# First attention head prepared inside the query projection, later heads fetched two ahead: a diffusion trunk on one core

## The chip, the cores and the metric

The kernel runs on one core of one Trainium2 chip. The metric is the device time of one execution, in microseconds (us). All times below are in us from the start of the profiled span unless another unit stands there.

## What is computed

A trunk of two layers over 512 latent and 256 context tokens (together T = 768) of width 1024. Each layer projects its modulated input once; the columns feed three groups of heads (RWKV time mixing, attention, mLSTM), whose outputs are projected back together, and a SwiGLU feed-forward follows. The change touches the attention group and its neighbour, the mLSTM. Attention has 8 heads with keys of 96 channels; a query is projected from a normalized latent `cq`, normalized per head, rotated, and goes against all keys:

```
ql, kl, vl = project(zl, True)     # latent tokens, rotated
qc, kc, vc = project(zc, False)    # context tokens
keys = concat([kl, kc]); vals = concat([vl, vc])
s = einsum(q, keys) * (MLA_QK ** -0.5); p = softmax(s); out = einsum(p, vals)
out_c = attend(qc, kc, vc)         # only in the first layer
```

In the first layer queries are formed for all 768 tokens, in the last for the 512 latent ones.

## The kernel before

All matmul work that must be accurate is split in two parts, hi and lo, and takes three passes (L246 to L248, L1028 to L1030). The program is written with pools of tiles; a list scheduler decides the order on each engine from the program's dependences, and then every engine executes its list in order. DMAs go out from SP's list, also in order. A tile's memory or PSUM bank is handed to the next tile of the same name, in program order, when the last reader is done.

In each layer, after the RWKV scan, `mla_up` forms keys, queries and values while `mlstm` works on the side. `heads` projects pairs of token tiles (`up`, PSUM tile `up`, two of them), normalizes and rotates, and `by_channel` transposes four heads at a time into the PSUM tile `bc` (L904), ScalarE copies them to `stg` (L906, three buffers), and SP writes them to DRAM, to `ktd` or `qtd` (L907). First come the keys of all heads, then the queries of heads 0 to 3 (a = 0), then those of heads 4 to 7 (a = 1), then the values (`up` of 512 columns, stored in three pages, L969).

`mla_attend` then takes the heads one after the other. `load` reads a head's keys and queries from DRAM into a staging tile `kq` (two of them) and splits each: ScalarE rounds to hi (L993, L990), GpSimd (keys, L994) or VectorE (queries, L991, with the gain) forms lo. `maxima` finds the largest score of each query for the softmax: two matmuls into `mx` (L1008), a VectorE reduce (L1010), and after four query tiles a transposition into `pt` (L1014) and a copy to row 96 of the queries (L1015). `attend` forms the scores of 128 keys by 512 or 256 queries (`st`, L1028 to L1030), ScalarE takes the exponential (L1032), a matmul with the values adds to `po` (L1034). The first range of a head holds query tiles 0 to 3 against all keys, the second, only in the first layer, tiles 4 and 5 against the context's keys. At a range's end ScalarE copies the row of sums (L1039). The maxima of the next head are interleaved with the current one's keys, and its load is issued at the current one's start. After each of seven heads one piece of `rwkv_post` follows. The mLSTM's outputs lie in a page `hs` and its finish transposes them into `pss` (L1307).

Of the kernel before, what the change touches and what calls it, by code (L numbers as in the profile page):

```python
# [11 lines left out]
F32 = mybir.dt.float32  # L12
F32R = mybir.dt.float32r
# [13 lines left out]
POST = (0, 0, 0, 0, 0)  # L27
# [149 lines left out]
def trunk(ctx, tc, I, out, dbg=None):  # L177
# [662 lines left out]
    def mla_up(l, ctx_out, lat, wk, pm, krt, post, marks):  # L840

        steps = iter(POST)

        def fill():
            for _ in range(next(steps, 0)):
                next(post, None)
# [105 lines left out]
        fill()  # L952
        for n in range(0, NT, 2):
            heads(ckv, rkv, wt, n, n + 2, 8, 64, (kr2[:, :, 0], ks), ktd, 0)
            fill()
        for a in range(2):
            wt = up_weight("uq", 4, 384 * a, 384 * a + 384)
            for n in range(0, nq // P, QN):
                heads(cq, rq, wt, n, min(n + QN, nq // P), 4, 96, None, qtd, 4 * a)
            fill()  # L960
# [11 lines left out]
    def mla_attend(l, ctx_out, y, V, wk, wk2, pm, pv, post):  # L972
        nq = T if ctx_out else TL
        psum = lambda: pm.tile([P, 512], F32, name="mx")
# [5 lines left out]
        ac.activation(idr, ident, AF.Copy)  # L980

        def load(h):

            r = []
            for src, i, n in ((ktd, 1, T), (qtd, 0, nq)):
                t = wk.tile([96, T], F32, name="kq", bufs=2)[:, :n]
                dma = sp.dma_start(out=t, in_=src[h, :, :n])
                hi, lo = (w.tile([97, T], F32R, name=f"k{i}{j}", bufs=2)[:, :n] for j, w in enumerate((wk, wk2)))
                if i == 0:
                    ac.activation(hi[0:96], t, AF.Copy, scale=gain)  # L990
                    ve.scalar_tensor_tensor(lo[0:96], t, gain, hi[0:96].bitcast(F32), ALU.mult, ALU.subtract)  # L991
                else:
                    ac.activation(hi[0:96], t, AF.Copy)  # L993
                    gp.tensor_tensor(lo[0:96], t, hi[0:96].bitcast(F32), ALU.subtract)  # L994
                    gp.memset(hi[96:97].bitcast(F32), 1.0)
                r += [hi, lo]
            loads.append(dma)
            return r

        def maxima(kq, q0, q1, k0):  # L1000
            kh, kl, qh, ql = kq
            w = q1 - q0
            mr = wk.tile([P, 4], F32R, name="mr")
            for n in range(q0, q1):
                ps = pm.tile([P, 1024], F32, name="mx", bufs=1)
                for a, b in ((0, 512), (512, T)):
                    if a >= k0:
                        pe.matmul(ps[:, a - k0:b - k0], qh[0:96, n * P:(n + 1) * P], kh[0:96, a:b],  # L1008
                                  start=True, stop=True)
                ve.tensor_reduce(mr[:, n - q0:n - q0 + 1], ps[:, :T - k0], AX.X, ALU.max)  # L1010
                yield
            pt = pm.tile([P, 512], F32, name="pt")
# [3 lines left out]
            yield  # L1016

        def attend(h, kq, q0, q1, k0):
# [21 lines left out]
            pd = pm.tile([P, 512], F32, name="pt")  # L1040
# [4 lines left out]
            bc = pm.tile([P, 512], F32, name="pt")  # L1045
# [6 lines left out]
        ranges = ((0, 4, 0), (4, 6, 512))[:2 if ctx_out else 1]  # L1052
        loads, done = [], []
        kq = load(0)
        for _ in maxima(kq, *ranges[0]):
            pass
        for h in range(8):
            ahead = [maxima(kq, *g) for g in ranges[1:]]
            if h < 7:
                kq2 = load(h + 1)  # L1060
                ahead.append(maxima(kq2, *ranges[0]))
            ahead = chain(*ahead)
            for g in ranges:
                for _ in attend(h, kq, *g):
                    next(ahead, None)
# [6 lines left out]
            kq = kq2  # L1072
# [109 lines left out]
    def mlstm(l, ctx_out, y, qk, wk, pm, Q, rp):  # L1182
# [30 lines left out]
        hs = hp.tile([P, NT, 256], F32, name="hpage")  # L1213
# [9 lines left out]
        def chunk(d, i, n):  # L1223
# [12 lines left out]
            if has_y:  # L1236
# [34 lines left out]
                hv = hs[:, n].rearrange("p (h b) -> p h b", b=64)  # L1271
                rb = r.to_broadcast([P, 4, 64])
                if n in seen:
                    t = wk.tile([P, 4, 64], F32, name="m1")
                    ve.tensor_tensor(t, pn[:, :, 0:64], rb, ALU.mult)
                    gp.tensor_tensor(hv, hv, t, ALU.add)
                else:
                    seen.add(n)
                    ve.tensor_tensor(hv, pn[:, :, 0:64], rb, ALU.mult)
# [13 lines left out]
        def finish(ns):  # L1293

            st = wk.tile([P, 2, 8], F32, name="mst")
            for i, n in enumerate(ns):
                sq = wk.tile([P, 256], F32, name="m1")
                ac.activation(sq, hs[:, n], AF.Square)
                ve.tensor_reduce(st[:, 0, 4 * i:4 * i + 4], sq[:, :].rearrange("p (h b) -> p h b", b=64), AX.X, ALU.add)
            ve.tensor_scalar(st[:, 0], st[:, 0], 1.0 / 64, EPS, ALU.mult, ALU.add)  # L1300
            rsqrt(st[:, 1], st[:, 0], 8, "m")
            for i, n in enumerate(ns):
                hv = hs[:, n].rearrange("p (h b) -> p h b", b=64)
                ve.tensor_tensor(hv, hv, st[:, 1, 4 * i:4 * i + 4].unsqueeze(2).to_broadcast([P, 4, 64]), ALU.mult)
                ps = pm.tile([P, 512], F32, name="pss")
                for j in range(2):
                    pe.transpose(ps[:, j * P:(j + 1) * P], hs[:, n, j * P:(j + 1) * P], ident)  # L1307
# [79 lines left out]
    for l in range(DEPTH):  # L1387
# [24 lines left out]
        wp2 = rstack.enter_context(pool(f"po{l}", 2, "right"))  # L1412
        lstack = ExitStack()
        wm = lstack.enter_context(pool(f"ml{l}", 2, "right"))
        with pool(f"pb{l}", 1, space=PSUM) as psb, pool(f"pu{l}", 2, space=PSUM) as pm, \
                pool(f"mu{l}") as wk:
            marks = mlstm(l, ctx_out, y, qk, wm, psb, Q, rp)
            psum = [lambda: pm.tile([P, 512], F32, name="bc")]
            post = rwkv_post(l, ctx_out, data, y, wp2, psum)
            V = mla_up(l, ctx_out, lat, wk, pm, krt, post, marks)  # L1420
        lstack.close()
        with pool(f"ma{l}") as wk, pool(f"mb{l}") as wk2, pool(f"pv{l}", 2, space=PSUM) as pv, pool(f"pa{l}", 2, space=PSUM) as pm:
            psum[0] = lambda: pm.tile([P, 512], F32, name="pt")
            loads, marks = mla_attend(l, ctx_out, y, V, wk, wk2, pm, pv, post)
# [105 lines left out]
```

## Time and profile before

| | |
|---|---|
| runs shown | 2282.0 median of 3 (2281.18 to 2285.35) |
| profiled execution | 2283.55, span 2281.8 |
[...]
| busy: TensorE, VectorE, ScalarE, GpSimd | 2159.2, 1381.9, 844.7, 314.2 |
| TensorE waiting for the split of head 0 before its first maxima, layer 0 | 6.1 |

The page gives totals, costliest groups and the chain of work that ended last. The place of the change is short against the span, so it is read from views of a stretch: the chain of waits in it, a table by windows, and lists of single instructions. In a list, x2 behind a row means two instructions in a row, and brackets name what the engine had waited for. The engines are PE (TensorE), DVE (VectorE), ACT (ScalarE), POOL (GpSimd) and SP.

### The profile page before, as it was taken

To read this page: it belongs to the slowest core of one execution; us is meant where nothing else is said; L and a number is where in the kernel's file an instruction comes from. 1 tells how busy PE (TensorE), PEld (TensorE's weight loads), DVE (VectorE), ACT (ScalarE), POOL (GpSimd) and SP (SyncE) were. 2 spreads that over 40 slices of the span, in tenths; PEclk is the share of its full clock that TensorE was granted. 3 is DMA by queue.
4 is the path that set the end of the run, shared out by engine and by line. 5 is a ranking of instruction groups with operands and counts; after the bars stand their busy time and mean duration, and the time that the engine had idled before them with its cause. 6 is when DMAs were issued, how large, how long until landed. Compare 5 with 4: busy or idle time off the path is not lost.

```text
span 2281.8 us, 36365 instructions
## 1 busy us (share of the span) xinstructions
PE 2159.2 (95%) x14604; PEld 1780.9 (78%) x14604; DVE 1381.9 (61%) x2706; ACT 844.7 (37%) x1527; POOL 314.2 (14%) x482
## 2 busy tenths in 40 slices
PE   7999997997999999999999999999898998999999
PEld 4788886784668788888888878787685677888887
DVE  6687777895547766554444455788796545334343
ACT  4433333664552421122122354433473544222231
POOL 1022322332201100000000111113142211000000
PEclk9999997897999999999999989999697998999999
DMA  7241112232115334344432312211232122323323
GB/s 289 84 153 52 62 41 74 77 88 56 42 70 155 100 114 146 111 129 135 133 112 83 109 52 63 73 57 39 85 100 59 35 74 83 101 94 94 100 92 102
DMA packets 87352, 211.99 MB, mean 93 GB/s; under 512 B 10248, under 2 KB 33680, under 8 KB 86544
## 3 DMA queue, kind: packets, MB, share of 16 engines
q1 hardware_dynamic: 87184, 209.67, 29.2%
q8 instruction: 115, 1.88, 0.3%
q14 instruction: 53, 0.43, 0.1%
HBM read 187.62 MB, written 22.02 MB: 92 GB/s over the span
## 4 chain that ended last, share of the span: by engine, by line
PE 81%; DVE 10%; ACT 4%; DMA 2%; issue 2%; POOL 1%; SPq 0%; DVEq 0%; ACTq 0%; POOLq 0%
PE gm L262 57%; PE po L1034 4%; PE psm L585 2%; PE inv L660 2%; PE st L1028 1%; DVE cT L320 1%; PE st L1029 1%; PE st L1030 1%; PE mx L1008 1%; PE psm L514 1%; PE pB L700 1%; DVE wl L228 1%; PE psm L573 1%; ACT hu L365 1%; PE up L246 1%
## 5 line engine op out<-in xcount | busy, mean ns | idle before, releaser
L262 PE MATMUL gm<-hpage,wh 128*128 128x512 f32 (+1 forms) x3744 | 1001.7, 355 | 15.3 <-ACT hpage L227 8.9
L262 PEld LDWEIGHTS gm<-hpage,wh 128*128 128x128 f32 x3744 | 664.2, 191 | 119.8 <-ACT hpage L227 11.0
L262 PE MATMUL gm<-hpage,wl 128*128 128x512 f32 (+1 forms) x1872 | 657.4, 353 | 1.9 <-DVE wl L228 1.8
L227 ACT ACTIVATE wh<-wr 128x1024 fp32r<-128x1024 f32 (+2 forms) x214 | 221.6, 1036 | 560.7 <-PE gm L262 457.6
L262 PEld LDWEIGHTS gm<-hpage,wl 128*128 128x128 f32 x1872 | 358.1, 191 | 50.6 <-DVE wl L228 2.5
L228 DVE TENSOR_TENSOR wl<-wr,wh 128x1024 fp32r<-128x1024 f32 (+2 forms) x214 | 258.2, 1207 | 186.9 <-ACT wh L227 185.1
L262 PE MATMUL gm<-hid,wh 128*128 128x512 f32 (+1 forms) x1056 | 282.6, 356 | 0.0
L262 PEld LDWEIGHTS gm<-hid,wh 128*128 128x128 f32 x1056 | 185.6, 188 | 32.2
L262 PE MATMUL gm<-hid,wl 128*128 128x512 f32 (+1 forms) x528 | 187.4, 356 | 0.0
L1323 DVE SCALAR_TENSOR_TENSOR X<-gm,mod,X 128x512 f32<-128x512 f32 (+1 forms) x100 | 64.0, 643 | 191.0 <-PE gm L262 187.7
L320 DVE CUSTOM_DVE_ANT_0 cT<-wd,cB,mod_b 128x1024 f32<-128x1024 f32 x140 | 177.7, 1300 | 1.1 <-DMA wd<-in_mod_d 0.7
L1492 DVE SCALAR_TENSOR_TENSOR ft<-ft,gm 128x512 f32<-128x512 f32 x66 | 39.5, 598 | 153.0 <-PE gm L262 152.7
L1010 DVE TENSOR_REDUCE mr<-mx 128x1 fp32r<-128x768 f32 (+1 forms) x80 | 67.9, 848 | 83.8 <-PE mx L1008 83.6
L1034 PE MATMUL po<-pe,hpage 128*128 128x512 f32 (+1 forms) x224 | 112.2, 590 | 0.5 <-ACT pe L1032 0.4
L262 PEld LDWEIGHTS gm<-hid,wl 128*128 128x128 f32 x528 | 99.0, 188 | 16.1
L338 POOL TENSOR_TENSOR acc<-acc,sq 128x512 f32<-128x512 f32 (+1 forms) x15 | 23.9, 1601 | 604.0 <-ACT sq L337 604.0
L1032 ACT ACTIVATE pe<-st 128x512 f32<-128x512 f32 (+1 forms) x112 | 62.9, 563 | 89.8 <-PE st L1030 88.7
L227 ACT ACTIVATE hid<-ft 128x512 fp32r<-128x512 f32 x66 | 36.2, 549 | 128.4 <-DVE ft L1492 128.4
L1028 PE MATMUL st<-k,k 97*128 97x512 f32 (+1 forms) x112 | 78.0, 698 | 4.7 <-ACT k L1015 4.1
L1490 ACT ACTIVATE ft<-gm 128x512 f32<-128x512 f32 x66 | 33.9, 514 | 90.4 <-PE gm L262 90.3
L1008 PE MATMUL mx<-k,k 96*128 96x256 f32 (+1 forms) x144 | 46.3, 396 | 17.1 <-DVE mr L1010 9.9
L585 PE MATMUL psm<-pr,kb 64*128 64x128 f32 (+1 forms) x384 | 57.7, 308 | 1.4 <-POOL pr L555 1.4
(425 smaller groups left out, 3128.5 us busy)
## 6 DMA issues: line engine op xcount, KB each, us to landing
wr<-in_ffn_in SPq DMA_DIRECT2D x88, 512.0 KB, 3.5
wd<-in_mod_d SPq DMA_DIRECT2D x86, 512.0 KB, 3.8
wr<-in_w_in SPq DMA_DIRECT2D x44, 512.0 KB, 3.6
wr<-in_ffn_out SPq DMA_DIRECT2D x34, 448.0 KB, 3.4
wr<-in_w_out SPq DMA_DIRECT2D x20, 512.0 KB, 3.7
wr<-in_ffn_out SPq DMA_DIRECT2D x16, 512.0 KB, 3.6
zs<-ze SPq DMA_DIRECT2D x26, 256.0 KB, 2.0
X<-in_xT SPq DMA_DIRECT2D x16, 384.0 KB, 6.4
```

What stands on the lines that cost most here:

```text
L227: ac.activation(hi, src, AF.Copy)
L228: return en.tensor_tensor(lo, src, hi.bitcast(F32), ALU.subtract)
L262: pe.matmul(ps, x[:, j], act[k][y][:, a:b], start=(i == 0 and n == 0), stop=(i == len(kl) - 1 and n == 2))
L320: ve.tensor_tensor_reduce(out=t[:, s], in0=w, in1=cb[:, s], scale=1.0, scalar=modb[:, l, m:m + 1], op0=ALU.mult, op1=ALU.add, accum_out=mo ...
L585: pe.matmul(pa[j][:, p, c], flat(kb[hr, d, p, c]), flat(pr[hr, d, p, c, 0:nq]), start=True, stop=True)
L660: i = pe.matmul(v8(o)[hr, q], a[hr, d, p, c], b[hr, d, p, c], start=True, stop=True)
L1008: pe.matmul(ps[:, a - k0:b - k0], qh[0:96, n * P:(n + 1) * P], kh[0:96, a:b], start=True, stop=True)
L1010: ve.tensor_reduce(mr[:, n - q0:n - q0 + 1], ps[:, :T - k0], AX.X, ALU.max)
L1028: pe.matmul(ps, kh[0:97, ks], qh[0:97, qs], start=True, stop=False)
L1032: ac.activation(e, ps, AF.Exp, scale=QK_SCALE)
L1034: pe.matmul(po[:, :w], v, e, start=(kt == kts[0]), stop=(kt == kts[-1]))
L1323: return ve.scalar_tensor_tensor(X[:, m, a:b], ps, mods[l][:, 24 * which + 16 + m, s:s + 1], X[:, m, a:b], ALU.mult, ALU.add)
```

## The change

`mla_heads` now holds `load` and `maxima`, and a function `between` is called by `mla_up` after the queries of heads 0 to 3. It loads head 0's keys into a page (`hpage`) and its queries into a tile `qs` of a pool that is opened for it, splits them and takes the maxima of the first range, in the PSUM tiles `up` (512 and 256 columns apart, so eight reduces in place of four, and a maximum over the two) and `bc`. The load goes straight into the lo half of the tile, ScalarE forms hi from it, and lo is formed in place; the staging tile `kq` is gone. The keys and queries of later heads have three buffers, `ks` and `qs`, and are fetched two heads ahead. The mLSTM's outputs are stored in a part of `y`, which frees the page. The pool of `rwkv_post` (its loads of `g2` and `gz` among it) moves behind the mLSTM, and the pools of attention's PSUM tiles change places. Calls that were switched off (POST) are gone.

```diff
@@ mla_up
             for n in range(0, nq // P, QN):
                 heads(cq, rq, wt, n, min(n + QN, nq // P), 4, 96, None, qtd, 4 * a)
-            fill()
+            if a == 0:
+                between()
...
@@ mla_heads (new; load and maxima moved here)
+        def load(h, k, q):
+            kh, kl, qh, ql = k[0:97, 0], k[0:97, 1], q[0:97, 0, :nq], q[0:97, 1, :nq]
+            raw = lambda t: t[0:96].bitcast(F32)
+            sp.dma_start(out=raw(kl), in_=ktd[h])
+            ac.activation(kh[0:96], raw(kl), AF.Copy)
+            gp.tensor_tensor(kl[0:96], raw(kl), raw(kh), ALU.subtract)
+            gp.memset(kh[96:97].bitcast(F32), 1.0)
+            loads.append(sp.dma_start(out=raw(ql), in_=qtd[h, :, :nq]))
+            ac.activation(qh[0:96], raw(ql), AF.Copy, scale=gain)
+            ve.scalar_tensor_tensor(ql[0:96], raw(ql), gain, raw(qh), ALU.mult, ALU.subtract)
+            return kh, kl, qh, ql
...
             for n in range(q0, q1):
+                ps = None if mx is None else mx()
+                for i, (a, b) in enumerate(rng):
+                    p = psum("up")[:, :b - a] if mx is None else ps[:, a - k0:b - k0]
+                    pe.matmul(p, qh[0:96, n * P:(n + 1) * P], kh[0:96, a:b], start=True, stop=True)
+                    if mx is None:
+                        ve.tensor_reduce(m2[:, i, n - q0:n - q0 + 1], p, AX.X, ALU.max)
...
+            pt = psum("bc" if mx is None else "pt")
...
@@ mla_attend
-        kq = load(0)
-        for _ in maxima(kq, *ranges[0]):
-            pass
+        fetch = lambda h: load(h, wk.tile([P, 2, T], F32R, name="ks", bufs=3), wk2.tile([P, 2, T], F32R, name="qs", bufs=3))
+        kqs = {0: kq, 1: fetch(1)}
         for h in range(8):
-            ahead = [maxima(kq, *g) for g in ranges[1:]]
+            kq = kqs.pop(h)
+            ahead = [maxima(kq, *g, mx, psum) for g in ranges[1:]]
             if h < 7:
-                kq2 = load(h + 1)
-                ahead.append(maxima(kq2, *ranges[0]))
+                ahead.append(maxima(kqs[h + 1], *ranges[0], mx, psum))
+            if h < 6:
+                kqs[h + 2] = fetch(h + 2)
...
@@ mlstm
-        hs = hp.tile([P, NT, 256], F32, name="hpage")
+        hs = [y[:, 6:8, n * P:(n + 1) * P] for n in range(NT)]
...
@@ layer
-        wp2 = rstack.enter_context(pool(f"po{l}", 2, "right"))
+        qp = rstack.enter_context(pool(f"q{l}", 1, "right"))
+        heads, kq = mla_heads(l, ctx_out, qp), []
...
+            def between():
+                kq.append(heads[0](0, hp.tile([P, 2, T], F32R, name="hpage"), qp.tile([P, 2, T], F32R, name="qs")))
+                for _ in heads[1](kq[0], *RANGES[0], None, lambda name: pm.tile([P, 512], F32, name=name)):
+                    pass
+            V = mla_up(l, ctx_out, lat, wk, pm, krt, marks, between)
...
-        with pool(f"ma{l}") as wk, pool(f"mb{l}") as wk2, pool(f"pv{l}", 2, space=PSUM) as pv, pool(f"pa{l}", 2, space=PSUM) as pm:
+        with pool(f"po{l}") as wp2, pool(f"ma{l}") as wk, pool(f"mb{l}") as wk2, pool(f"pa{l}", 2, space=PSUM) as pm, pool(f"pv{l}", 2, space=PSUM) as pv:
```

The change moves instructions on every engine. TensorE's order in layer 0 of the kernel before, from the last values matmuls to the first scores (`bc` are transposed query pairs, `pss` the mLSTM's finish, `mx` the maxima):

```order
L248 MATMUL up<-wh,hpage 128x512
L904 MATMUL bc<-c_id,kn 96x128 x8
L1307 MATMUL pss<-c_id,hpage 128x128 x6
L1008 MATMUL mx<-k_5829,k_5836 128x512
L1008 MATMUL mx<-k_5829,k_5836 128x256
...
L1014 MATMUL pt<-idr,mr 128x128 x2
L1008 MATMUL mx<-k_5829,k_5836 128x256
L1028 MATMUL st<-k_5836,k_5829 128x512
```

And now, from the last query pair of heads 0 to 3 to the first matmuls of heads 4 to 7 (of 384 columns); `pn` and `pbc` are the mLSTM's chunks:

```order
L1236 MATMUL pbc<-c_id,sb 128x128
L898 MATMUL bc<-c_id,kn 96x128 x8
L1267 MATMUL pn<-C_4509,qd 128x260
L1270 MATMUL pn<-mva,m_4998 128x65 x4
...
L1270 MATMUL pn<-mva,m_5031 128x65 x4
L1313 MATMUL pss<-c_id,y 128x128 x2
L1002 MATMUL up<-hpage,qs 128x512
L1002 MATMUL up<-hpage,qs 128x256
L1313 MATMUL pss<-c_id,y 128x128 x2
...
L245 MATMUL up<-wh,hpage 128x384
L246 MATMUL up<-wl,hpage 128x384
```

Head 0's maxima stood between the values and the first scores, and stand now between the two halves of the query projection; all matmuls of heads 4 to 7 and of the values follow them, and the first scores follow the last `bc` directly.

ScalarE's order at the start of attention in layer 0, before (`kq` to `k` are the splits of heads 0 and 1, `pe` the exponentials):

```order
L906 ACTIVATE stg<-bc 96x512 x2
L980 ACTIVATE idr<-c_id 128x128
L993 ACTIVATE k_5829<-kq 96x768
L990 ACTIVATE k_5836<-kq,qkgain 96x768
L993 ACTIVATE k_5865<-kq 96x768
L990 ACTIVATE k_5872<-kq,qkgain 96x768
L1015 ACTIVATE k_5836<-pt 1x512
L1032 ACTIVATE pe<-st 128x512 x4
```

And now (`ks` are the keys of heads 1 and 2, then 3):

```order
L900 ACTIVATE stg<-bc 96x512 x2
L1036 ACTIVATE pe<-st 128x512 x2
L983 ACTIVATE ks<-ks 96x768 x2
L1036 ACTIVATE pe<-st 128x512 x2
L983 ACTIVATE ks<-ks 96x768
L1036 ACTIVATE pe<-st 128x512 x2
```

The splits of head 0 are gone from the start, and the copies of two later heads' keys stand between the second and the third exponential.

SP's order now, from the load of head 0's keys on (head 0's queries and those of heads 1 to 3 are the x4):

```order
L982 DMA hpage<-ktd 96x768
L901 DMA qtd<-stg 96x4x128 x2
L234 DMA wr<-in_ukv 128x2x512
L901 DMA qtd<-stg 96x4x128 x2
L234 DMA wr<-in_w_out 128x1024
L901 DMA qtd<-stg 96x4x128 x2
L986 DMA qs<-qtd 96x768 x4
L901 DMA qtd<-stg 96x4x128 x2
L234 DMA wr<-in_w_out 128x1024 x2
L901 DMA qtd<-stg 96x4x128 x4
L234 DMA wr<-in_w_out 128x1024
L982 DMA ks<-ktd 96x768 x2
```

All loads of a head stood behind the last query write; now the queries of four heads are read before the second half is written, while the keys of heads 1 and 2 still stand behind it.

## Rows read from the trace of the kernel before

**Rows 1.** The page: busy time of TensorE, share of the span, instructions; shares of the chain.

```profile
PE 2159.2 (95%) x14604; PEld 1780.9 (78%) x14604; DVE 1381.9 (61%) x2706; ACT 844.7 (37%) x1527; POOL 314.2 (14%) x482
...
PE 81%; DVE 10%; ACT 4%; DMA 2%; issue 2%; POOL 1%; SPq 0%; DVEq 0%; ACTq 0%; POOLq 0%
```

**Rows 2.** Chain of waits, layer 0, 509 to 535: start us, us, what.

```profile
509.43 0.23 PE up L247
...
509.90 0.87 PE bc L904 x8
...
514.04 6.21 DMA kq<-ktd
...
521.06 0.94 ACT k L990
...
523.85 3.23 DMA kq<-qtd
...
533.86 0.76 PE st L1028
```

**Rows 3.** Table by windows: stretch, length, busy us (and instructions) by engine, PEclk, DMA share, GB/s.

```profile
390.00:400.00 10.00, 4.95 (x68) 4.01 (x68) 7.02 (x15) 2.48 (x4) 1.27 (x5) 0.63 0.70 223
400.00:410.00 10.00, 9.42 (x85) 7.87 (x86) 6.74 (x13) 5.59 (x10) 1.33 (x1) 0.50 0.43 150
520.00:530.00 10.00, 3.24 (x8) 2.16 (x8) 6.02 (x8) 3.50 (x4) 3.62 (x2) 0.50 0.24 65
```

**Rows 4.** List of TensorE's instructions, layer 1, at 1738: start us, us, engine, line, operation.

```profile
1738.44 1.19 PE L1028 MATMUL st<-k,k 97*128 97x512 f32 x2 [0.16 <-ACT k L1015]
```

**Rows 5.** Lists of ScalarE's (row L1039) and TensorE's instructions, heads of both layers.

```profile
547.58 0.59 ACT L1039 ACTIVATE row<-po 1x512 f32<-1x512 f32 x1 [0.42 <-PE po L1034]
...
566.28 0.59 ACT L1039 ACTIVATE row<-po 1x512 f32<-1x512 f32 x1 [0.63 <-PE po L1034]
...
582.65 0.59 ACT L1039 ACTIVATE row<-po 1x512 f32<-1x512 f32 x1 [0.42 <-PE po L1034]
...
586.44 0.47 PE L1028 MATMUL st<-k,k 97*128 97x512 f32 x1 [0.58 <-ACT k L1015]
...
599.08 0.59 ACT L1039 ACTIVATE row<-po 1x512 f32<-1x512 f32 x1 [0.76 <-PE po L1034]
...
1753.87 0.59 ACT L1039 ACTIVATE row<-po 1x512 f32<-1x512 f32 x1 [0.60 <-PE po L1034]
...
1772.47 0.59 ACT L1039 ACTIVATE row<-po 1x512 f32<-1x512 f32 x1 [0.61 <-PE po L1034]
...
1786.12 0.59 ACT L1039 ACTIVATE row<-po 1x512 f32<-1x512 f32 x1 [0.60 <-PE po L1034]
```

**Rows 6.** List of SP's DMA issues: the query writes of both layers.

```profile
487.69 3.40 SPq L907 DMA_DIRECT2D qtd<-stg  x4
...
1706.05 1.35 SPq L907 DMA_DIRECT2D qtd<-stg  x2
```

**Rows 7.** DMA issues from 465 to 535: count, KB each, median us to landing.

```profile
qtd<-stg SPq DMA_DIRECT2D x12, 192.0 KB, 2.3
...
kq<-ktd SPq DMA_DIRECT2D x3, 288.0 KB, 4.6
kq<-qtd SPq DMA_DIRECT2D x3, 288.0 KB, 3.2
```

**Rows 8.** Groups of VectorE's instructions by shape, 425 to 560: busy us, mean ns.

```profile
L1010 DVE TENSOR_REDUCE mr<-mx 128x1 fp32r<-128x768 f32 x9 | 8.6, 953 | 11.8 <-PE mx L1008 11.8
...
L991 DVE SCALAR_TENSOR_TENSOR k<-kq,qkgain,k 96x768 fp32r<-96x768 f32 x3 | 4.3, 1449 | 2.9 <-ACT k L990 2.9
...
L1010 DVE TENSOR_REDUCE mr<-mx 128x1 fp32r<-128x256 f32 x4 | 1.7, 421 | 4.5 <-PE mx L1008 4.5
```

**Rows 9.** List of TensorE's instructions, second half of the query projection, layer 0.

```profile
485.40 0.33 PE L247 MATMUL up<-wl,hpage 128*128 128x384 f32 x1
...
485.75 0.33 PE L246 MATMUL up<-wh,hpage 128*128 128x384 f32 x1
```

More of the change, by code (lines that the diff above doesn't have):

```diff
@@ L26 @@
 EB = 6
-POST = (0, 0, 0, 0, 0)
 POSTA = (1, 1, 1, 1, 1, 1, 1, 0)
@@ L838, in latent, with mla_up @@
         return parts, rs
[L840 to L846, printed above, removed]
+    def mla_up(l, ctx_out, lat, wk, pm, krt, marks, between):
         nq = T if ctx_out else TL
@@ L970, in mla_up, with mla_heads @@
         return V
-    def mla_attend(l, ctx_out, y, V, wk, wk2, pm, pv, post):
+    RANGES = ((0, 4, 0), (4, 6, 512))
+    def mla_heads(l, ctx_out, wk):
         nq = T if ctx_out else TL
-        psum = lambda: pm.tile([P, 512], F32, name="mx")
         qkg = const("qkg", wk)
@@ L980, in mla_attend @@
         ac.activation(idr, ident, AF.Copy)
[L982 to L998, printed above, removed]
@@ L1000, in maxima @@
-        def maxima(kq, q0, q1, k0):
+        loads = []
+        def load(h, k, q):
[9 more added lines that the diff above has]
+            return kh, kl, qh, ql
@@ L1001, in maxima @@
+        def maxima(kq, q0, q1, k0, mx, psum):
             kh, kl, qh, ql = kq
             w = q1 - q0
-            mr = wk.tile([P, 4], F32R, name="mr")
+            mr = wk.tile([P, 4], F32R, name="mr", bufs=2)
+            rng = [(a, b) for a, b in ((0, 512), (512, T)) if a >= k0]
+            m2 = wk.tile([P, 2, 4], F32, name="m2", bufs=1) if mx is None else None
             for n in range(q0, q1):
[L1005 to L1010, printed above, removed]
+                ps = None if mx is None else mx()
[4 more added lines that the diff above has]
+                        ve.tensor_reduce(m2[:, i, n - q0:n - q0 + 1], p, AX.X, ALU.max)
+                if mx is not None:
+                    ve.tensor_reduce(mr[:, n - q0:n - q0 + 1], ps[:, :T - k0], AX.X, ALU.max)
@@ L1011, in maxima @@
                 yield
-            pt = pm.tile([P, 512], F32, name="pt")
+            if mx is None:
+                ve.tensor_tensor(mr[:, :w], m2[:, 0, :w], m2[:, 1, :w], ALU.max)
+            pt = psum("bc" if mx is None else "pt")
             for n in range(w):
@@ L1016, in maxima, with mla_attend @@
             yield
+        return load, maxima, loads
+    def mla_attend(l, ctx_out, y, V, heads, kq, wk, wk2, pm, pv, post):
+        load, maxima, loads = heads
+        psum = lambda name: pm.tile([P, 512], F32, name=name)
+        mx = lambda: pm.tile([P, 1024], F32, name="mx", bufs=1)
         def attend(h, kq, q0, q1, k0):
@@ L1039, in attend @@
             ac.activation(row, po[o:o + 1, :w], AF.Copy)
-            pd = pm.tile([P, 512], F32, name="pt")
+            pd = psum("pt")
             for n in range(q1 - q0):
@@ L1044, in attend @@
             ve.reciprocal(r[:, :q1 - q0], pd[:, :q1 - q0])
-            bc = pm.tile([P, 512], F32, name="pt")
+            bc = psum("pt")
             for n in range(q1 - q0):
@@ L1278, in chunk @@
                     seen.add(n)
-                    ve.tensor_tensor(hv, pn[:, :, 0:64], rb, ALU.mult)
+                    ve.tensor_tensor(hv, nv, rb, ALU.mult)
             if i == NT - 1:
@@ L1417, in trunk @@
             marks = mlstm(l, ctx_out, y, qk, wm, psb, Q, rp)
-            psum = [lambda: pm.tile([P, 512], F32, name="bc")]
-            post = rwkv_post(l, ctx_out, data, y, wp2, psum)
-            V = mla_up(l, ctx_out, lat, wk, pm, krt, post, marks)
+            def between():
[3 more added lines that the diff above has]
+            V = mla_up(l, ctx_out, lat, wk, pm, krt, marks, between)
         lstack.close()
-        with pool(f"ma{l}") as wk, pool(f"mb{l}") as wk2, pool(f"pv{l}", 2, space=PSUM) as pv, pool(f"pa{l}", 2, space=PSUM) as pm:
-            psum[0] = lambda: pm.tile([P, 512], F32, name="pt")
-            loads, marks = mla_attend(l, ctx_out, y, V, wk, wk2, pm, pv, post)
+        with pool(f"po{l}") as wp2, pool(f"ma{l}") as wk, pool(f"mb{l}") as wk2, pool(f"pa{l}", 2, space=PSUM) as pm, pool(f"pv{l}", 2, space=PSUM) as pv:
+            post = rwkv_post(l, ctx_out, data, y, wp2, [lambda: pm.tile([P, 512], F32, name="pt")])
+            loads, marks = mla_attend(l, ctx_out, y, V, heads, kq[0], wk, wk2, pm, pv, post)
         rstack.close()
```

25 lines of the change are left out of this document (12 added, 13 removed).

## The prediction

> **What bounds the kernel now.** I read the page first: TensorE is busy for 95% of the span and the chain that ends last runs over it for 81% [rows 1]. So a microsecond is won only where TensorE stands idle or runs slowly, and I looked for such places next to the code that changes. The chain of waits around the start of attention in layer 0 shows one: the transposes of the last query pair (bc) are issued at 509.90 and the first score matmul (st) at 533.86, and between them stand the DRAM round trip of head 0 (keys 6.21, queries of head 1 3.23), the splits and the maxima [rows 2]. In this stretch VectorE and ScalarE wait too; it is latency and not work. [...] In layer 1 the first st comes at 1738.44 [rows 4].
>
> The list of ScalarE's instructions gives the heads, by the copy of the sums' row that ends each head's first range. Layer 0: the first head takes 547.58 − 533.86 = 13.7, the second 18.7, the third 16.4. Layer 1: 15.4, 18.6, 13.65 [rows 4, 5]. An undisturbed head needs 599.08 − 586.44 = 12.6 from its first st to its row [rows 5]. [...]
>
> **The change, term by term.** All sums are in the profiled execution's own time, 2283.55; the median of the runs shown, 2282.0, is 1.55 lower. A measurement of this kernel tells 0.2%, 4.6 us, from no change.
>
> *1. First st of layer 0.* The round trip of head 0 isn't removed, it is moved between the two halves of the query projection. The maxima now write into the PSUM tiles named up and bc, and these are handed out in program order: the matmuls of the second half stand behind the maxima in TensorE's order and need the same two up tiles. So TensorE still waits for the trip, but with four chunks of the mLSTM to work on. When does the trip end? The queries of the last pair of the first half are written at 487.69 [rows 6]; the new order has that pair at about the same place, so I take 487.5. The write lands 2.3 later, the read of a head's queries 3.2 later [rows 7], ScalarE's half of the split takes 0.94 [rows 2], VectorE's 1.45, and then eight reduces in place of four: 0.95 for 768 columns and 0.42 for 256 [rows 8], so about 0.68 for 512 and 1.1 per tile, 4.4 in all. That is 499.9; VectorE has mLSTM work between, for which I add 1: 501. Behind it TensorE has 72 matmuls of the second half at 0.175 (two steps between starts in 0.35 [rows 9]), 36 for the values at 0.23 and 24 transposes at 0.11 (0.87 for eight) [rows 2], and 1.5 for the mLSTM's last transposes and the second range's maxima: 12.6 + 8.3 + 2.6 + 1.5 = 25. First st at 526 against 533.86. The bounds: a trip with the same contention as the chain shows (6.21 in place of 3.2) gives 529; a trip wholly inside the mLSTM's work, with the second half beginning at 495, gives 520.
>
> After the hold the clock has to be reckoned with. A stretch in which TensorE works little is followed by one at 0.50: at 390 to 400 it is busy for 4.95, and from 400 to 410 the clock is 0.50, though the engine is busy for 9.42 [rows 3]. Between nothing and 10 us at half rate, that is between 0 and 5 us lost, I take 2 a layer, nearer the low end, since the mLSTM's matmuls go on during the hold. [...] With 2: first st at 528.3, **−5.5**.
>
> *2. The first head of layer 0.* It now begins at full clock behind dense matmuls, 12.6. But it gets a new wait. The keys of head 2 are read behind the last query writes, because their new tile takes over memory of stg, and ScalarE has the copies of heads 1 and 2 ahead of its third exponential. From the last eviction, which also releases the first st: write 2.3, read 4.6 [rows 7], two copies 0.9 each: the third exponential at about 8 after the first st, where it would come at about 4.5. That holds ScalarE, then TensorE, for 3.3. What is queued behind it: the remaining exponentials, and with them every po matmul. With 0.3 for the clock, 16.2 against 13.7: **+2.5**. Bounds: 0 if the reads are as short as 3.2 and the copies overlap; +6 with a read of 6.21 and a restart at half rate.
>
> *3. The second head of layer 0.* Its loads come two heads ahead, so it costs a steady 16.4 and not 18.7: **−2.3**. A low clock behind the stall of term 2 could eat this, so 0 to −2.3.
>
> *4. Layer 1, first st.* The second pair of the first half is written at 1706.05 [rows 6]; without the second half's matmuls among it I take 1704. Then 2.3 for the write, 3.9 for the read (the middle of 3.2 and 4.6) [rows 7], 2 for the split, 4.4 for the reduces: 1716.6. Behind it 48 × 0.175 + 36 × 0.23 + 16 × 0.11 + 1.5 = 19.9, and 2 for the clock: 1738.5, and 1 more because the mLSTM ends late in this layer and VectorE was busy nearly to the first st. 1739.6 against 1738.44: **+1.2**, between −6 and +6.
>
> *5. Layer 1, first and second head.* 16.2 against 15.4 is **+0.8** (from −2.8 to +4.3, as term 2), and 13.7 against 18.6 is **−4.9** (0 to −4.9).
>
> *6. The small edits.* The gain and the maxima's bias are computed from the same number of columns; eight more reduces (2 x 4 x 0.15) lie in terms 1 and 4. The g2 and gz loads move behind the keys' loads and are used only in the second head; covered by term 2's wait, and without that cover one load of about 4. The mLSTM keeps its outputs in y and not in a page: same counts and same columns, so nothing. From the third head on the order of TensorE and ScalarE is nearly the old one, nothing. X is still loaded behind the fourth head's loads, and the weights of wd go ahead of it on SP's queue; the out-projection starts on y, so nothing, at worst one load of 4.
>
> Sum: −5.5 + 2.5 − 2.3 + 1.2 + 0.8 − 4.9 = **−8.2**. 2283.55 − 8.2 = 2275.35, on the median's footing 2273.8; I say **2274**.
>
> **The rivals.**
>
> *The hold vanishes.* If the mLSTM's chunks cover the trip wholly in both layers, the first st follows the last bc: about 512 in layer 0 (−22), and about 1732 in layer 1, where VectorE's remaining work sets it (−6). With terms 2, 3 and 5 as above: −22 + 0.2 − 6 − 4.1 = −32, so 2250. For it: the order puts mLSTM chunks into the gap. Against it: all of the second half's 72 matmuls stand behind the maxima, so 25 us of TensorE remain after the trip whatever covers it. Chance 0.07.
>
> *Moved, not won.* Terms 1, 2, 4 and 5 each lean to their dear ends by some 2: the read of head 0's queries shares the queues with 512 KB of w_out, as in the chain of before, and ScalarE waits for the third head's queries before the value weights are split. −8.2 + 4 × 2 = 0, so 2282. For it: the total wait per layer is the same DRAM trip twice, and term 2 adds a new one. Chance 0.23.
>
> *Slower by the clock.* [...] At 17 of the 25 us in each layer it is 8.5 and not 2, −8.2 + 13 = +4.8 in the profiled time: 2288, on the median's footing 2287; that is the point from which it is slower by more than 0.2%. [...] Chance 0.12.
>
> *The fetch two ahead does nothing,* if the copies' places in ScalarE's order hold it back: then terms 3 and 5 lose their 7.2 and the time is 2281. It counts with "moved, not won".
>
> **How the numbers follow.** The forecast, from 2262 to 2277.4, has 0.58, so faster by over 0.2% (under 2277.4) has 0.58 + 0.07 = 0.65. Within 0.2% has 0.23 and slower 0.12. The range reaches down to where about half of the first rival is out, 2259, and up to 2287, where the slower rival begins; some 0.15 is left out.
>
> **What would show it.** Right: the st that followed ACT k at 533.86 follows the last stg at 526 to 530; in 490 to 501 VectorE's reduces from up tiles, and the second half's first matmul waits for one; the third exponential of the first head waits for a copy of keys, which waits for a DMA from ktd; rows of head 2 − head 1 near 16.4 and 13.7. Wrong: second-half matmuls before 495; the first head at 12.6 without an idle ScalarE (better); a granted clock under 0.7 in 500 to 515 or 1716 to 1730 (worse); or heads from the third on that differ by over 0.3 each, which no term here explains.

## The result and the profile after

The changed kernel is slower: 2305.09 us (median of 4, 2298.69 to 2312.87) against 2283.68 (2281.18 to 2286.15), ratio 1.0097 with the interval 1.0076 to 1.0118. The forecast was 2274, with 2287 as the upper end of the range. The profiled execution is the slowest of the four, 2312.87, span 2310.9, 29.1 longer than the span of before.

The page of the changed kernel, busy time and shares of the chain, answers to [rows 1]:

```profile
PE 2179.3 (94%) x14604; PEld 1793.4 (78%) x14604; DVE 1381.1 (60%) x2716; ACT 846.9 (37%) x1527; POOL 311.1 (13%) x482
...
PE 80%; DVE 10%; DMA 4%; ACT 4%; issue 2%; SPq 0%; POOL 0%; ACTq 0%; DVEq 0%; POOLq 0%
```

The amount of work is the same, 14604 matmuls; TensorE's busy time grew by 20.1 and the span by 29.1. To see where, I take three marks in each layer from the lists of TensorE's instructions: the first matmul of the key projection (up), the first scores (st) and the first matmul of the output projection (gm). The kernel before, the marks not shown above:

```profile
422.08 0.48 PE L246 MATMUL up<-wh,hpage 128*128 128x512 f32 x1
...
673.20 0.96 PE L262 MATMUL gm<-hpage,wh 128*128 128x512 f32 x4 [0.29 <-ACT hpage L227]
...
1654.82 0.48 PE L246 MATMUL up<-wh,hpage 128*128 128x512 f32 x1
...
1854.35 0.70 PE L262 MATMUL gm<-hpage,wh 128*128 128x512 f32 x2
```

The changed kernel:

```profile
424.70 0.48 PE L245 MATMUL up<-wh,hpage 128*128 128x512 f32 x1
...
536.61 0.50 PE L1032 MATMUL st<-qs,hpage 97*128 97x512 f32 x1 [1.81 <-ACT stg L900]
...
681.26 0.96 PE L261 MATMUL gm<-hpage,wh 128*128 128x512 f32 x4 [1.13 <-ACT hpage L226]
...
1663.01 0.48 PE L245 MATMUL up<-wh,hpage 128*128 128x512 f32 x1
...
1756.24 0.50 PE L1032 MATMUL st<-qs,hpage 97*128 97x512 f32 x1 [1.29 <-ACT stg L900]
...
1882.70 0.50 PE L261 MATMUL gm<-hpage,wh 128*128 128x512 f32 x1 [0.85 <-DVE y L1054]
```

From the first up to the first st it is 111.8 before [rows 2] and 111.9 now in layer 0, 83.6 [rows 4] and 93.2 in layer 1. From there to gm it is 139.3 and 144.7 in layer 0, 115.9 and 126.5 in layer 1. The stretch from gm of layer 0 to up of layer 1 is 981.6 and 981.8. So layer 1 costs some 20 and layer 0 some 5.5; 2.6 lie ahead of the first up and 0.7 after the last gm. The medians differ by 21.4 and not by 29.1; in which stretch this execution is slower than the median one isn't known.

The copies of the sums' row that end the first heads, as in [rows 5]:

```profile
554.14 0.59 ACT L1043 ACTIVATE row<-po 1x512 f32<-1x512 f32 x1 [0.42 <-PE po L1038]
...
571.91 0.59 ACT L1043 ACTIVATE row<-po 1x512 f32<-1x512 f32 x1 [0.47 <-PE po L1038]
...
1769.86 0.59 ACT L1043 ACTIVATE row<-po 1x512 f32<-1x512 f32 x1 [1.59 <-PE po L1038]
```

The first head takes 17.5 in layer 0 and 13.6 in layer 1 (13.7 and 15.4 before), the second 17.8 and 18.8 (18.7 and 18.6).

**The hold in layer 1.** The chain of waits of the changed kernel, 1690 to 1800 (start, us, what):

```profile
1714.05 1.72 PE bc L898 x8
...
1716.41 2.18 DMA qtd<-stg
1718.73 2.38 DMA qs<-qtd
...
1726.94 1.03 PE pn L1267 x2
...
1730.88 0.69 PE up L245
...
1740.97 1.07 ACT wh L226
...
1743.32 0.35 SPq L234
1743.71 4.71 DMA qs<-qtd
...
1750.53 0.50 PE up L245
```

The last query pair of heads 0 to 3 is transposed at 1714.05, written and read again, and only at 1730.88 does the second half start: 16.8 us. Between the maxima (up L1002 in the chain) stands a chunk of the mLSTM (pn). After this comes a second hold that I hadn't priced: SP's queue waits at 1743.32 to issue a load of w_out into a buffer that VectorE must free first, the queries of heads 1 to 3 stand behind it (4.71), and ScalarE has their copies ahead of a values copy (hpage), so TensorE's next values matmul of the chain starts at 1750.53, after 0.98 of idle time.

The clock in the holds (table by windows, columns as in [rows 3]):

```profile
500.00:510.00 10.00, 7.81 (x24) 6.21 (x25) 7.55 (x27) 1.07 (x3) 0.72 (x1) 0.55 0.00 0
...
1720.00:1730.00 10.00, 8.48 (x29) 6.90 (x30) 7.69 (x32) 1.33 (x3) 2.16 (x4) 0.54 0.05 16
...
1740.00:1750.00 10.00, 9.29 (x46) 7.25 (x44) 8.53 (x27) 6.71 (x11) 2.01 (x3) 1.00 0.56 160
```

The granted clock was 0.55 in 500 to 510 and 0.54 in 1720 to 1730, though TensorE was busy for 7.81 and 8.48 of 10, and it was back at 1.00 by 1740. So TensorE had the low clock during the hold itself, while it worked on the mLSTM. The second half of layer 1 starts with it too: its first matmuls follow each other at 0.32, with a granted clock of 0.50 in 1730 to 1734, the later ones at 0.175, with 1.00 in 1735 to 1740.

**The second half in layer 0.** VectorE's list shows the splits of three later heads' queries inside the projection, among the second half's own work:

```profile
518.48 1.58 DVE L988 SCALAR_TENSOR_TENSOR qs<-qs,qkgain 96x768 fp32r<-96x768 f32 x1
...
521.12 1.00 DVE L988 SCALAR_TENSOR_TENSOR qs<-qs,qkgain 96x768 fp32r<-96x768 f32 x1
...
522.12 1.01 DVE L988 SCALAR_TENSOR_TENSOR qs<-qs,qkgain 96x768 fp32r<-96x768 f32 x1
```

**The first head of layer 0.** ScalarE's list:

```profile
537.60 1.29 ACT L1036 ACTIVATE pe<-st 128x512 f32<-128x512 f32 x2 [1.05 <-PE st L1034]
543.99 0.84 ACT L983 ACTIVATE ks<-ks 96x768 fp32r<-96x768 f32 x1 [5.10 <-DMA ks<-ktd]
545.23 0.84 ACT L983 ACTIVATE ks<-ks 96x768 fp32r<-96x768 f32 x1 [0.39 <-DMA gz<-zs]
545.98 1.06 ACT L1036 ACTIVATE pe<-st 128x512 f32<-128x512 f32 x2
```

The third exponential (the row of 545.98, two of them) waits for two key copies, and the first of these for a DMA, 5.10. This is the new wait of term 2.

**The later heads of layer 1.** ScalarE's list at the end of the second head:

```profile
1784.47 0.60 ACT L1036 ACTIVATE pe<-st 128x512 f32<-128x512 f32 x1 [1.42 <-PE st L1034]
1787.79 0.84 ACT L983 ACTIVATE ks<-ks 96x768 fp32r<-96x768 f32 x1 [2.73 <-DMA ks<-ktd]
1788.66 0.59 ACT L1043 ACTIVATE row<-po 1x512 f32<-1x512 f32 x1
```

The keys that are fetched two ahead are copied directly in front of the row copy, after a wait of 2.73 for their DMA. The row copy needs nothing from it and had no idle time of its own before it: it stood behind. The chain of waits shows what the DMA itself waited for, the last score matmul that reads the tile's old contents:

```profile
1784.20 0.24 PE st L1034
1784.51 3.20 DMA ks<-ktd
1787.79 0.84 ACT ks L983
1788.66 0.60 ACT row L1043
```

SP's queue says the same for the heads of layer 1 (its waits: us in total, times, longest):

```profile
SPq L982 <- PE st L1034: 67.6, 4, 22.0
```

The same pattern follows at later heads; summed over the heads of layer 1 (waits of ScalarE: us in total, times, longest):

```profile
ACT ks L983 <- DMA ks<-ktd: 11.2, 7, 2.7
```

The kernel before has no such wait behind the first head of layer 1: its DMA went to a staging tile.

### The profile page after: what moved, and what is told of

Read it like the earlier page. It is cut to its first block, busy times and chain, and to the rows that moved or that the text cites. A ratio compares the mean times of both kernels' runs of the same rounds, so it can differ in the third digit from the quotient of the medians.

```text
span 2310.9 us, 36349 instructions
## 1 busy us (share of the span) xinstructions
PE 2179.3 (94%) x14604; PEld 1793.4 (78%) x14604; DVE 1381.1 (60%) x2716; ACT 846.9 (37%) x1527; POOL 311.1 (13%) x482
## 4 chain that ended last, share of the span: by engine, by line
PE 80%; DVE 10%; DMA 4%; ACT 4%; issue 2%; SPq 0%; POOL 0%; ACTq 0%; DVEq 0%; POOLq 0%
PE gm L261 57%; PE po L1038 4%; PE psm L584 2%; PE inv L659 2%; DVE cT L319 1%; PE st L1032 1%; PE psm L513 1%; PE st L1033 1%; PE st L1034 1%; PE pB L699 1%; DMA wd<-in_mod_d 1%; PE mx L1002 1%; DVE wl L227 1%; PE psm L572 1%; PE up L245 1%
## 5 line engine op out<-in xcount | busy, mean ns | idle before, releaser
L261 PEld LDWEIGHTS gm<-hpage,wh 128*128 128x128 f32 x3744 | 663.8, 191 | 120.5 <-ACT hpage L226 11.8
L1006 DVE TENSOR_REDUCE mr<-mx 128x1 fp32r<-128x768 f32 (+1 forms) x72 | 60.2, 836 | 101.8 <-PE mx L1002 101.7
L1032 PE MATMUL st<-qs,ks 97*128 97x512 f32 (+1 forms) x98 | 68.8, 702 | 3.5 <-ACT qs L1013 3.5
L1038 PEld LDWEIGHTS po<-pe,hpage 128*128 128x128 f32 x224 | 39.9, 202 | 19.6 <-ACT pe L1036 12.0
```

Of the source, the lines that this page charges most:

```text
L261: pe.matmul(ps, x[:, j], act[k][y][:, a:b], start=(i == 0 and n == 0), stop=(i == len(kl) - 1 and n == 2))
L1032: pe.matmul(ps, kh[0:97, ks], qh[0:97, qs], start=True, stop=False)
L1038: pe.matmul(po[:, :w], v, e, start=(kt == kts[0]), stop=(kt == kts[-1]))
```

## The experiments

Twelve kernels, each a variation of the changed one. Since the list scheduler orders the whole program anew, an edit here can move instructions far away: of the 2458 matmuls of the RWKV scan in layer 1, the changed kernel, `head0_late`, `late_staged` and `late_one` have 6 to 12 at another place than the kernel before, the others 697 to 1382. So besides the ratio I give the stretches that the edit is about, from the marks above in each profiled execution: up to st, and st to gm, layer 0 / layer 1; and between, gm of layer 0 to up of layer 1. They come from one execution each: among the five kernels with nearly the same order of the scan, between spreads from 975.9 to 981.8, so a few us in one stretch decide nothing.

| run | head 0 prepared | later heads | ratio (95%) | up to st | st to gm | between |
|---|---|---|---|---|---|---|
| before | after values, from DRAM | one ahead, staged | 1 | 111.8 / 83.6 | 139.3 / 115.9 | 981.6 |
| changed | between halves, up | two, in place | 1.0097 (1.0076–1.0118) | 111.9 / 93.2 | 144.7 / 126.5 | 981.8 |
| head0_late | behind values, up | two, in place | 0.9986 (0.9970–1.0001) | 100.1 / 80.1 | 142.5 / 124.8 | 977.9 |
| one_ahead | between halves, up | one, in place | 1.0147 (1.0125–1.0169) | 107.5 / 91.2 | 139.3 / 141.9 | 985.3 |
| late_one | behind values, up | one, in place | 1.0034 (1.0008–1.0060) | 104.6 / 78.0 | 136.3 / 142.1 | 975.9 |
| v_first | values, then head 0 | two, in place | 1.0152 (1.0118–1.0186) | 118.2 / 97.6 | 136.9 / 126.9 | 988.1 |
| late_staged | behind values, up | one, staged | **0.9909** (0.9880–0.9938) | 101.9 / 78.3 | 137.2 / 115.2 | 978.3 |
| mid_staged | between halves, up | one, staged | 0.9996 (0.9983–1.0009) | 107.8 / 87.0 | 142.8 / 111.4 | 980.1 |
| after_a1 | after second half, up | two, in place | 1.0046 (1.0029–1.0064) | 104.2 / 81.0 | 142.6 / 129.4 | 983.1 |
| late_staged_2a | behind values, up | two, staged | 0.9951 (0.9937–0.9965) | 102.1 / 79.0 | 139.5 / 116.2 | 986.3 |
| after_bc | between halves, bc | two, in place | 1.0055 (1.0030–1.0081) | 103.3 / 79.3 | 143.0 / 123.3 | 983.0 |
| mid_staged_2a | between halves, up | two, staged | 1.0057 (1.0039–1.0075) | 111.5 / 88.2 | 141.7 / 113.4 | 985.7 |
| late_staged_two | behind values, up | DMA two, split one, staged | 0.9953 (0.9935–0.9971) | 105.9 / 77.3 | 137.6 / 113.7 | 981.3 |
| bc_staged | between halves, bc | one, staged | 0.9979 (0.9959–1.0000) | 102.9 / 78.3 | 140.3 / 114.2 | 986.1 |

Theory 1 at first: the time goes to the hold between the halves and to the fetch two ahead. The rival: to the moved pools, PSUM tiles and loads.

**head0_late**: head 0 behind the values.

```diff
-            if a == 0:
-                between()
...
+        between()
         return V
```

> Head 0's loads, splits and maxima are put behind the value matmuls in program order; the fetch two ahead stays. If the hold between the two halves of the query projection is what costs (theory 1: the time goes to this hold, to the key copies in the first head and to the copies of the keys two ahead that stand before the row copies), the second half's matmuls start at once, the first st of layer 1 comes some 8 us earlier against that layer's start and the ratio to the kernel before is 1.003 to 1.007 (changed kernel: 1.0097). If it is the surroundings (theory 2: moved pools, PSUM tiles, moved loads), the ratio stays at 1.010.

0.9986, better than expected: the first st come 11.8 and 13.1 earlier than in the changed kernel. The place of head 0 alone turns 1.0097 into no loss. The heads stay long (124.8 in layer 1).

**one_ahead**: the fetch undone.

```diff
-        fetch = lambda h: load(h, wk.tile([P, 2, T], F32R, name="ks", bufs=3), wk2.tile([P, 2, T], F32R, name="qs", bufs=3))
-        kqs = {0: kq, 1: fetch(1)}
+        fetch = lambda h: load(h, wk.tile([P, 2, T], F32R, name="ks", bufs=2), wk2.tile([P, 2, T], F32R, name="qs", bufs=2))
+        kqs = {0: kq}
...
             kq = kqs.pop(h)
+            if h < 7:
+                kqs[h + 1] = fetch(h + 1)
...
-            if h < 6:
-                kqs[h + 2] = fetch(h + 2)
```

> The preparation of head 0 inside the projection stays, later heads are fetched one ahead with two buffers. Theory 1: ScalarE's waits for keys from DRAM in heads 2 to 7 (7.7 us in layer 0, 11.2 in layer 1) shrink to a few us, the heads from the third on come back to 16.4 and 13.7, and the ratio falls to 1.000 to 1.004, the hold in layer 1 staying. If the fetch is innocent (theory 2, or all loss in the hold), the ratio stays at 1.008 to 1.010.

A miss, and the wrong way: 1.0147. The heads of layer 1 grow to 141.9, and ScalarE's waits for keys from DRAM with them:

```profile
ACT ks L983 <- DMA ks<-ktd: 19.6, 7, 4.4
```

So it is not the fetch two ahead that holds ScalarE. It softens something that one ahead shows in full.

**late_one**: both edits together.

> Both undone: head 0 is prepared behind the values and later heads are fetched one ahead; left over are the in-place split without a staging tile, the mLSTM's outputs in y, the moved pools and PSUM tiles. Theory 1: no slower than the kernel before, ratio 0.995 to 1.001. Theory 2: the loss stays, 1.005 to 1.010.

1.0034, in neither range, so neither theory holds as it stood: a loss of 0.3% stays with both undone, and it lies in the heads of layer 1 (142.1 against 115.9; every other stretch of the table is shorter than before). What is left there of the change is the load straight into the lo half. That made the new theory 1: a tile that is loaded in place can be loaded only when its last reader is done, so the trip from DRAM falls between the release and the copy, and the copy stands in ScalarE's order ahead of work that is ready. In the changed kernel these waits are the 67.6 of SP's queue for the last reader and the 11.2 of ScalarE for the trip, in layer 1.

**v_first**: the values between the first half and head 0.

```diff
             if a == 0:
+                wt = up_weight("ukv", 2, 512, 1024)
+                for n in range(NT):
+                    ps = up(ckv, wt, n, 512)
+                    ac.activation(V[n][:, :, 0:64], ps.rearrange("p (h b) -> p h b", h=8), AF.Copy, scale=rkv[:, n:n + 1])
                 between()
```

> The value matmuls (36 in each layer, 8 us of TensorE) are put between the first half of the query projection and the preparation of head 0, so that they cover the DRAM trip; the fetch two ahead stays. Theory 1: TensorE has no wait over 2 us between the halves, the first st of layer 1 comes 5 to 9 us earlier against its layer's start, ratio 1.003 to 1.006, the rest being the fetch. If the DRAM trip is not the hold's cause (VectorE's reduces or the weights), no change: 1.009 to 1.010.

A miss: 1.0152. Moving dense matmuls into the trip made the first st later (118.2 / 97.6): the second half then stands alone at the end. In the changed kernel the values matmuls run beside VectorE's work on the second half, of which they need little. That this is the reason is argued, not shown.

**late_staged**: head 0 behind the values, one ahead, and the staging tiles back.

```diff
-            sp.dma_start(out=raw(kl), in_=ktd[h])
-            ac.activation(kh[0:96], raw(kl), AF.Copy)
-            gp.tensor_tensor(kl[0:96], raw(kl), raw(kh), ALU.subtract)
+            t, u = (wk.tile([96, T], F32, name="kq", bufs=2)[:, :n] for n in (T, nq))
+            sp.dma_start(out=t, in_=ktd[h])
+            loads.append(sp.dma_start(out=u, in_=qtd[h, :, :nq]))
+            ac.activation(kh[0:96], t, AF.Copy)
+            gp.tensor_tensor(kl[0:96], t, kh[0:96].bitcast(F32), ALU.subtract)
...
```

> Head 0 behind the values; later heads one ahead with two buffers, but loaded through the two staging tiles as in the kernel before. Against the run with both parts undone (1.0034) only the staging differs. Theory 1 (now): loading straight into the lo half ties the DMA to the moment when the head's old tile comes free, and ScalarE waits for the DMA with the copy ahead of a row copy; with staging the heads of layer 1 come back from 17.8 to 19.5 to about 13.7, attention of layer 1 from 133.8 to about 116, ratio 0.994 to 0.997. Theory 2 (PSUM tiles or moved loads slow the heads): heads of layer 1 stay over 16, ratio over 1.000.

0.9909, faster than the kernel before and the lowest ratio of all, though the intervals of `late_staged_2a` and `late_staged_two` below touch its own. Against `late_one` only the staging differs: layer 1's heads come from 142.1 to 115.2 (the 133.8 of the expectation counts from a later st than the first). Within the heads ScalarE waits for no keys any more; one wait, 6.90 for head 1's keys, ends at 1716.21, ahead of the first st at 1717.72. At a head's end its list now reads

```profile
1763.85 0.59 ACT L1047 ACTIVATE row<-po 1x512 f32<-1x512 f32 x1 [0.18 <-PE po L1042]
1764.47 0.59 ACT L1017 ACTIVATE qs<-pt 1x512 fp32r<-1x512 f32 x1
```

with the row copy in its place and the row of the next head's maxima directly behind it. SP's loads of keys no longer wait for a score matmul but for the reader of the staging tile, VectorE's split (four of them; three others wait for a load):

```profile
SPq L980 <- DVE qs L992: 51.1, 4, 21.8
```

This kernel still has the moved pools, PSUM tiles and loads, so these bring no net loss. And it shows what the early preparation is worth without the hold. Head 0's keys and queries are read here (first two rows, SP's list) long before the kernel before reads them (last two):

```profile
465.73 0.31 SPq L980 DMA_DIRECT2D kq<-ktd  x1
490.91 0.32 SPq L981 DMA_DIRECT2D kq<-qtd  x1
...
514.04 0.42 SPq L987 DMA_DIRECT2D kq<-ktd  x1
514.56 0.37 SPq L987 DMA_DIRECT2D kq<-qtd  x1
```

The first st come 9.9 and 5.3 earlier than before. How much of this the early reads give wasn't tested apart.

**mid_staged**: the same with head 0 between the halves.

> The same with head 0 prepared between the halves of the projection, as in the changed kernel. Theory 1: its heads are as short as in the run with staging and head 0 behind the values, and the hold alone stays: first st of layer 1 some 8 us later against the start of the key projection than there, of layer 0 3 to 8; ratio 0.998 to 1.004. If the place of head 0 costs through the heads and not through the hold, the first st come within 3 us of each other.

The first st come 5.9 and 8.7 later than in `late_staged`; the heads of layer 1 are as short (111.4), those of layer 0 are longer by 5.6, which is the first head (19.4 against 13.6): a copy of keys ahead of its third exponential waits for its DMA, staging or not, as in term 2.

```profile
536.90 0.84 ACT L989 ACTIVATE ks<-kq 96x768 fp32r<-96x768 f32 x1 [4.80 <-DMA kq<-ktd]
```

0.9996: head 0 in this place eats all that the rest wins.

**after_a1**: `if a == 1` in place of `if a == 0`.

> The changed kernel with one number changed: head 0 is prepared after the second half of the query projection and before the values, so the trip has the second half's 72 or 48 matmuls ahead of it and the values behind it. Theory 1: the first half's trip has ended by then, the hold goes except for the reduces; first st within 3 us of the kernel with head 0 behind the values, ratio 0.998 to 1.003. If any preparation ahead of dense matmuls costs, it stays at 1.005 or more.

First st at 104.2 / 81.0, later than in `head0_late` by 4.1 and 0.9, so most of the hold is gone without the values ahead. The ratio 1.0046 is over the range of theory 1 and the 4.1 over its 3; the heads in place cost as before, and 5.2 of the whole lie in the stretch between (983.1 against 977.9), which this edit isn't about.

**late_staged_2a**: `late_staged` with the fetch two ahead and three buffers.

> Head 0 behind the values, fetch two ahead with three buffers, and the two staging tiles. Theory 1: DMAs land early whatever the fetch, so it is within 0.2% of the same kernel with one ahead (0.994 to 0.997). If the fetch two ahead has a worth of its own, beyond hiding the in-place load, it is faster by 0.3% or more.

A miss on the other side: 0.9951, slower than one ahead by 0.4% (the intervals touch). Of its 8.3 us in the profiled times 8.0 lie in the stretch between, where TensorE waits in the RWKV scan (waits of TensorE, 1440 to 1460), and `late_staged` has none of these:

```profile
PE pA L690 <- DVE st L703: 2.9, 1, 2.9
PE psm L598 <- DVE av L589: 1.8, 1, 1.8
```

I put this down to the other order of the scan and not to the fetch; the two waits are 4.7 of the 8.0, the rest isn't traced. The stretches of attention, at any rate, show nothing won by the fetch two ahead once staging hides the DMA.

**after_bc**: one word.

```diff
-                    p = psum("up")[:, :b - a] if mx is None else ps[:, a - k0:b - k0]
+                    p = psum("bc")[:, :b - a] if mx is None else ps[:, a - k0:b - k0]
```

> The changed kernel with one word changed: head 0's maxima are formed in the PSUM tiles named bc and no longer in those named up, which the matmuls of the second half need; its order has the second half's matmuls of layer 0 ahead of the maxima. Theory 1 (the hold is the handing out of up tiles): TensorE works on through the trip, the first st come 5 us or more earlier against the start of the key projection (before this 111.9 and 93.2), ratio 1.003 to 1.007; the losses in the heads stay. Theory 2 (the trip and VectorE's work bind, whatever tile): first st within 2 us, ratio 1.009 to 1.010.

As theory 1 said: the first st come 8.6 and 13.9 earlier than in the changed kernel, as early as with head 0 behind the values. TensorE's list shows the maxima waiting for head 0's queries once, 1.64, with values matmuls running until then, and the first st at 1729.07 (up at 1649.78):

```profile
1709.80 0.62 PE L1002 MATMUL bc<-hpage,qs 96*128 96x512 f32 x2 [1.64 <-ACT qs L987]
...
1729.07 0.50 PE L1032 MATMUL st<-qs,hpage 97*128 97x512 f32 x1 [0.98 <-ACT stg L900]
```

So the hold is neither the trip nor the place but the tile: the maxima took the PSUM tiles that the covering matmuls needed. `bc_staged` against `mid_staged` is the same edit once more: 4.9 and 8.7.

**mid_staged_2a**: the changed kernel with staging and nothing else.

> The changed kernel with the two staging tiles put back and nothing else. Theory 1: ScalarE's waits for keys from DRAM in the heads of layer 1 (11.2 us) go, its heads come to 13.7; the hold stays. Ratio 1.002 to 1.006. Theory 2 (staging matters only with two buffers, one ahead): ratio 1.008 or more.

1.0057: ScalarE's waits for keys in layer 1 fall from 11.2 to 1.0 and its heads from 126.5 to 113.4; the hold stays in the main (111.5 / 88.2).

**late_staged_two**: three staging tiles, DMAs two ahead, splits one ahead.

> Head 0 behind the values, two buffers and staging as in the fastest so far (0.9909), but three staging tiles and the DMAs issued two heads ahead, the splits one ahead. If the fetch two ahead has a worth when it holds no engine: 0.3% faster than that, 0.988. If the DMAs are hidden already by the staging tiles: the same within 0.2%.

0.9953, not faster, and 0.4% over `late_staged`, which neither theory said: the heads are those of `late_staged` (137.6 / 113.7), so nothing is left there for earlier DMAs to win.

**bc_staged**: both cures, head 0 where the change put it.

> Head 0 between the halves as in the changed kernel, but its maxima in the bc tiles; later heads one ahead, with staging. Theory 1: hold and in-place load are both gone, so it comes close to the fastest (0.989 to 0.995) although head 0 stands where the change put it. If preparing head 0 there costs in any PSUM tile: 0.998 to 1.001, as the same with up tiles (0.9996).

First st 102.9 / 78.3 and heads 140.3 / 114.2, both within 3.1 of `late_staged` or better. The ratio, 0.9979, misses my range; 7.8 of the difference lie in the stretch between (986.1 against 978.3). Its order of the scan is that of `v_first`, which has 988.1 there.

## Why the prediction was wrong

By its terms, in the profiled executions, each layer counted from its first up:

| term | said | measured |
|---|---|---|
| 1, first st, layer 0 | −5.5 | +0.1 |
| 2, first head, layer 0 | +2.5 | +3.8 |
| 3, second head, layer 0 | −2.3 | −0.9 |
| 4, first st, layer 1 | +1.2 | +9.6 |
| 5, first and second head, layer 1 | +0.8, −4.9 | −1.8, +0.2 |
| 6, from the third head on, layer 0, layer 1 | 0, 0 | +2.4, +12.2 |
| elsewhere | 0 | +3.4 |

Two of the prediction's signs of being wrong were there: a granted clock of 0.55 in 500 to 510 and 0.54 in 1720 to 1730, and heads from the third on that differ by more than 0.3.

**Term 6 failed most.** The prediction said that from the third head on the order is nearly the old one, nothing. The copies in that order waited for a DMA that they had not waited for: the staging tile that the change removed had let the DMA land early. I counted the load's instructions and not the moment from which the DMA may be issued. The runs show it in four pairs: with staging back, the heads of layer 1 fall by 26.9 (`late_one` to `late_staged`), 30.5 (`one_ahead` to `mid_staged`), 13.1 (changed to `mid_staged_2a`) and 8.6 (`head0_late` to `late_staged_2a`). In layer 0 the same pairs change by +0.9, +3.5, −3.0 and −3.0; why in-place loads cost so little there, I didn't test. Term 5's second head is not explained by this alone: 18.8 in the changed kernel, 18.2 in `mid_staged_2a` with staging back, 13.6 in `late_staged`.

**Term 4, and 1.** The mechanism was named rightly, up tiles handed out in program order, and `after_bc` shows it. Its size was wrong. In layer 1 the second half starts at 1730.88, which is 1722.7 on the clock of before (the layer starts 8.2 later), where I had 1716.6. Of these 6.1, 4.2 lie ahead of the write (1716.41, so 1708.2 and not 1704) and 2.9 in the reduces, which spread over 7.3 and not 4.4, with a chunk of the mLSTM among the maxima; the trip between was 1.0 shorter. Then the tail took 25.4 and not 22.9, the wait of SP and the queries of heads 1 to 3 in it. In layer 0 the hold ends at 505.80, 503.2 on the clock of before, where I had 501; the tail is 30.8 against 27, with three query splits on VectorE in it. (Term 1's own sum is 528.0 and −5.9; 528.3 and −5.5 stand there.) The prediction had these only in a rival, "moved, not won".

**The restart of the clock** was sized well: in layer 1 nine of the second half's matmuls take 0.32 and not 0.175, 1.3 us, where I had 2. The slower rival had the right sign and the wrong cause. It wanted 17 us at the low rate behind each hold, and no trace here shows them: in layer 1 the clock was back at 1734.45, 3.6 after the hold's end, and in layer 0, where the hold ends at 505.80, it was 0.50 in 506 to 508, 0.76 in 508 to 510 and 1.00 in 510 to 520.

**Term 2** was right: the third exponential came 9.4 after the first st (I said 8), with TensorE waiting 3.25 for the copies and 1.10 for the exponential. Its 0.3 for the clock no trace here shows by itself; the granted clock was 1.00 in 530 to 540 and 0.83 in 540 to 550. In layer 1 (term 5) the key copies stand behind the third exponential, TensorE waits 0.93 for the exponential behind them, and the first head takes 13.6 where I had 16.2.

**Term 3** came out at less than half, inside its bounds (0 to −2.3); what ate the rest wasn't tested.

What stays open is the 2.6 ahead of the first up in layer 0; in the experiments' profiles this mark lies between 419.7 and 425.9, so it may be no effect of the change.

## What to carry to other kernels

A staging tile that looks like a spare copy can be what lets a DMA go out early (with it back, the heads of layer 1 fell by 8.6 to 30.5 here): before it is removed, ask which reader now gates the DMA, and what stands behind the copy on its engine. A step that waits long should not take the PSUM tiles that the work meant to cover it needs; another tile's name brought the first scores of layer 1 forward by 13.9 us here. And where a scheduler orders the whole program, compare the stretch that an edit is about, since a whole-time ratio takes in reorderings elsewhere (the stretch between, which no edit here is about, lay up to 12 us apart). The idea of the change was good in another place: with head 0 prepared behind the values, staging kept and the later heads one ahead, the kernel is 0.9% faster than before.

## What was not expected

Waiting in order on ScalarE cost as much as it lasted, or more: ScalarE waited 11.2 for keys in layer 1's heads, and the stretch from st to gm grew by 10.6; in `one_ahead` it waited 19.6, and the stretch grew by 26.0. Yet ScalarE is busy for only 37% of the span. The row copy at 1788.66 shows how: the last matmul into its `po` ended at 1786.61, and it started 2.05 later, when the key copy ahead of it (1787.79, 0.84) had ended.

The four runs of the changed kernel spread over 14 us, the four of before over 5. This says little: 26 other runs of the kernel before spread over 21.
